# A two-layer decoder trunk: state-space output tables computed on VectorE into tiles of their own, table parts three steps apart, and Toeplitz gathers and V loads spread over a feed-forward stage

## The chip, the cores and the metric

One core of one Trainium2 chip runs the whole program. The metric is the device time of one execution in microseconds (us). Lower is better.

## The reference

Two layers act on x (256 rows of 1024 numbers, fp32). Each layer is a half-step SwiGLU feed-forward (ffn), a token mixer, a second ffn, and a gated embedding (ple). Layer 0 mixes with differential attention, layer 1 with a diagonal state-space model (ssm) and a gated linear unit (glu). Every sub-layer norms its input and its output.

```python
for i in range(2):
    x = x + 0.5 * rmsnorm(swiglu(rmsnorm(x, g[0]), ffn_w_in[i, 0], ffn_w_out[i, 0]), g[1])
    h = rmsnorm(x, g[2])
    m = diff_attention(h, ...) if i == 0 else s5_glu(h, ...)
    x = x + rmsnorm(m, g[3])
    x = x + 0.5 * rmsnorm(swiglu(rmsnorm(x, g[4]), ffn_w_in[i, 1], ffn_w_out[i, 1]), g[5])
    gate = sigmoid(rmsnorm(x, g[6]) @ ple_w_gate[i])
    x = x + rmsnorm(gate * (p[i] @ ple_w_proj[i]), g[7])
# in s5_glu, per group of 16 channels, with 64 complex states a = exp(lam * dt):
#   state = a * state + b_bar @ u ;  y = Re(c @ state) + d * u
```

## The kernel before, in words

**Stages and threads.** The eight stages are ffn(0,0), attention, ffn(0,1), ple(0), ffn(1,0), ssm with glu, ffn(1,1), ple(1). The 256 rows of x are two halves of 128, each worked on by a Python generator, thread 0 and thread 1 (`b` = 0 and 1). A step of a thread uses one weight tile. Thread 0 runs 4 to 7 steps ahead (`lags`), so that both use a tile while it is in SBUF. A scheduler orders the instructions on each engine once, when the program is built; on the chip each engine keeps that order. A block under `high_priority(offset=-800)` is placed with low priority, where an engine seems free.

**Weights.** A weight tile of 128x1024 fp32 is loaded by SP into one of three `raw` buffers. ScalarE rounds it to `hi` (L136), VectorE makes `lo = raw - hi` (L138). There are nine pairs of `hi` and `lo` (NB). A product takes three TensorE matmuls: hi·hi, lo·hi, hi·lo (L312 to L314). Each thread does two such triples of 128x512 with a tile, so a tile is 12 matmuls.

**Around a norm.** `post_norm` takes squares on ScalarE, a reciprocal root on GpSimd (`v_pn`, then `r_pn`, L323 and L327), and then adds to x on VectorE (L387). `pre_norm` transposes x on TensorE (`xT_ps`, L349) and evacuates with ScalarE (`xThi`) and VectorE (`xTlo`, L332). In ple, `mple` is gate times projection and `ygpnple` that times the gain, both on VectorE.

**Tables of the ssm.** While thread 1 runs through ffn(0,1), ple(0) and ffn(1,0), the main loop calls the generator `ssm_tables` at every second step. First come small tables on VectorE: powers of `a` (`ar`, `ai`), `er`, `ei`, then `br`, `bi`. Then, for each of eight group pairs `gp`:
- the v part: six products of 128x512 on GpSimd give `vr`, `vi`; four small GpSimd operations fill `cp`; TensorE transposes `vr`, `vi` (`v_ps`) in two sets of four and multiplies them with `cp` (`m_ps`); the results go to `v_d` in DRAM and to `msb`.
- the o part: six more GpSimd products give `or`, `oi`, in the same two SBUF buffers (tags `vr` and `vi`), stored to `o_d`.

After that `msb` gets a diagonal added (`db`, `dg`), is written to `m_d`, and eight DMAs from the GpSimd queue gather the Toeplitz table: `t_d <- m_d`, 512 KB each, in pieces of 512 bytes. When the generator ends, `load_v` loads four V tiles from `v_d`, 512 KB each, in one go. The ssm stage reads V, `t_d` and `o_d`.

Of the kernel before, what the change touches and what calls it, by code (L numbers as in the profile page):

```python
# [9 lines left out]
F32 = mybir.dt.float32  # L10
# [6 lines left out]
P = 128  # L17
# [49 lines left out]
STAGES = [("ffn", 0, 0), ("attn",), ("ffn", 0, 1), ("ple", 0),  # L67
          ("ffn", 1, 0), ("ssm",), ("ffn", 1, 1), ("ple", 1)]
TABLE_EVERY = OPT.get("every", 3)
PREPARE_AT = 36  # L70
EARLY = 24
LAMBDA_INIT = 0.8 - 0.6 * math.exp(0.0)
# [75 lines left out]
def trunk(ctx, tc, x, p, norm_g, ffn_w_in, ffn_w_out, attn_w_qkv, attn_w_o, attn_lam, attn_subln_g,  # L148
          rel_bias, ssm_lam_re, ssm_lam_im, ssm_log_dt, ssm_b_re, ssm_b_im, ssm_c_re, ssm_c_im, ssm_d, ssm_w_glu,
          ssm_b_glu, ple_w_proj, ple_w_gate, out):  # L150
    nc = tc.nc
# [21 lines left out]
    def bank(tag, name):  # L173
        return ps_extra["pool"].tile([P, 512], F32, tag=tag, name=name)
# [75 lines left out]
    if any(st[0] == "ssm" for st in stages):  # L250
        v_d = dram.tile([8, P, 1024], F32, name="v_d")
# [3 lines left out]
        t_d = dram.tile([P, 8, 1024], F32, name="t_d")  # L255
# [13 lines left out]
    plan = {}  # L269
# [9 lines left out]
    W = Weights(nc, raw_pool, split_pool, specs)  # L279
# [5 lines left out]
    def flat(u):  # L285
        return [u] if isinstance(u, int) else [a for e in u for a in flat(e)]
# [419 lines left out]
    ssm = {}  # L706
# [59 lines left out]
    def ssm_tables(pool, keep):  # L766
        lam, rho = ssm["lam"], ssm["rho"]
        v = nc.vector
        cnt = [0]

        def tmp(nm):
            return pool.tile([P, 32], F32, tag=f"s_{nm}", name=f"st_{nm}", bufs=1)
# [3 lines left out]
        n, y, z2, ps, pc = tmp("n"), tmp("y"), tmp("z2"), tmp("ps"), tmp("pc")  # L776
# [81 lines left out]
        for nm, src in (("re", ssm_b_re), ("im", ssm_b_im)):  # L858
            t = pool.tile([P, 32, 16], F32, tag="v" + nm[0], name=f"braw{nm}", bufs=1)
# [18 lines left out]
        for nm, src in (("re", ssm_c_re), ("im", ssm_c_im)):  # L878
            ct = pool.tile([P, 4, 8, 16], F32, tag=f"c{nm}", name=f"c{nm}", bufs=1)
            csrc = src[0].rearrange("(a g) h p -> (g h) a p", g=8)  # L880
            for hf in range(2):
# [3 lines left out]
                pt = bank("a1", f"c_ps{nm}{hf}")  # L885
# [15 lines left out]
        a4 = [t.rearrange("p k (q g) -> p q g k", q=4) for t in (ar, ai)]  # L901
        shp = [P, 4, 8, 16]

        def products(out_r, out_i, ar_, ai_, br_, bi_, nm):
            g = nc.gpsimd
            t = pool.tile([P, 512], F32, tag="pt", name=f"pt{nm}", bufs=1).rearrange("p (q k h) -> p q k h", q=4, k=8)
            g.tensor_tensor(out_r, ar_, br_, ALU.mult)
            g.tensor_tensor(t, ai_, bi_, ALU.mult)
            g.tensor_tensor(out_r, out_r, t, ALU.subtract)
            g.tensor_tensor(out_i, ai_, br_, ALU.mult)  # L910
            g.tensor_tensor(t, ar_, bi_, ALU.mult)
            g.tensor_tensor(out_i, out_i, t, ALU.add)

        zt = pool.tile([16, 112], F32, tag="vr", name="zt", bufs=1)
# [3 lines left out]
        for gp in range(8):  # L918
            vr = pool.tile(shp, F32, tag="vr", name=f"vr{gp}", bufs=1)
            vi = pool.tile(shp, F32, tag="vi", name=f"vi{gp}", bufs=1)  # L920
            A = [t[:, :, gp, 0:8].broadcast_to(shp) for t in a4]
            B = [t[:, :, gp:gp + 1, :].broadcast_to(shp) for t in b4]
            products(vr, vi, *A, *B, f"v{gp}")
            for e in range(2):
                sl = slice(64 * e, 64 * e + 64)
                nc.gpsimd.tensor_copy(cps[0][sl, :, e, :], c_re[sl, :, gp, :])
                nc.gpsimd.tensor_scalar(cps[1][sl, :, e, :], c_im[sl, :, gp, :], -1.0, None, ALU.mult)
            for i in range(2):
                vt = pool.tile([P, 2, 4, 64], F32, tag="cn", name=f"vt{gp}{i}", bufs=1)
                pt = bank("a0", f"v_ps{gp}{i}")  # L930
                for j in range(4):
                    q, ri = 2 * i + j // 2, j % 2
                    nc.tensor.transpose(pt[:, j * P:(j + 1) * P],
                                        (vr, vi)[ri][:, q].rearrange("p k h -> p (k h)"), ident)
                nc.scalar.copy(vt.rearrange("p e a n -> p a e n"), pt.rearrange("p (a e n) -> p a e n", a=4, e=2))
                nc.sync.dma_start(v_d[gp].rearrange("p (e a n) -> p e a n", e=2, n=64)[:, :, 4 * i:4 * i + 4, :], vt)
            mp = bank("a1", f"m_ps{gp}")
            for ri in range(2):
                for q in range(4):
                    nc.tensor.matmul(mp[32 * q:32 * q + 32, 0:P], cps[ri][:, q].rearrange("p e h -> p (e h)"),  # L940
                                     (vr, vi)[ri][:, q].rearrange("p k h -> p (k h)"), start=ri == 0, stop=ri == 1,
                                     skip_group_check=True)
            mt = work.tile([P, P], F32, tag="gnat", name=f"mt{gp}", bufs=1)
            nc.scalar.copy(mt, mp[:, 0:P])
            mp2 = bank("a0", f"m2_ps{gp}")
            nc.tensor.transpose(mp2[:, :P], mt, ident)
            nc.scalar.copy(msb[:, gp].rearrange("p e q h -> p q e h"), mp2[:, :P].rearrange("p (q e h) -> p q e h", q=4, e=2))
            yield
            o_r = pool.tile(shp, F32, tag="vr", name=f"or{gp}", bufs=1)
            o_i = pool.tile(shp, F32, tag="vi", name=f"oi{gp}", bufs=1)  # L950
            A = [t[:, :, gp, 1:9].broadcast_to(shp) for t in a4]
            C = [t[:, :, gp:gp + 1, :].broadcast_to(shp) for t in cs]
            products(o_r, o_i, *A, *C, f"o{gp}")
            for e in range(2):
                for ri, t in enumerate((o_r, o_i)):
                    nc.sync.dma_start(o_d[gp, ri * 64:ri * 64 + 64, e, :],
                                        t[64 * e:64 * e + 64].rearrange("p q t h -> p (q t h)"))
            yield

        m16 = msb.rearrange("p g e q h -> p (g e q) h")  # L960
        for q in range(4):
# [5 lines left out]
            v.tensor_tensor(db, db, ident[0:16, 0:16].rearrange("p (o h) -> p o h", o=1).broadcast_to([16, 16, 16]), ALU.mult)  # L967
            mq = msb.rearrange("p g e q h -> p (g e) q h")[0:16, :, q, :]
            v.tensor_tensor(mq, mq, db, ALU.add)
        yield 1  # L970
        for k in range(8):
            nc.gpsimd.dma_start(m_d[:, :, 7 + k, :], m16[16 * k:16 * k + 16])
        yield 2
        for s_ in range(8):
            nc.gpsimd.dma_start(t_d[16 * s_:16 * s_ + 16].rearrange("i g (c x) -> i (g c) x", x=P),
                              m_d.rearrange("i g k o -> i g (k o)")[:, :, 16 * s_:16 * s_ + P])
            yield 2


    def ssm_u(b):  # L980
# [238 lines left out]
    has_ssm = any(st[0] == "ssm" for st in stages)  # L1219
    pre = {"gen": None, "n": 0, "every": TABLE_EVERY}  # L1220

# [12 lines left out]
    def tables_step():  # L1234
        if pre["gen"] is not None:
            try:
                with tc.high_priority(offset=-PRE_OFFSET[min(pre["n"], len(PRE_OFFSET) - 1)]):
                    pre["every"] = next(pre["gen"]) or TABLE_EVERY
                pre["n"] += 1
# [5 lines left out]
    def load_v():  # L1245
        for pr in range(2):
            ssm["V", pr] = [ssm["pool"].tile([P, 1024], F32, tag=("bglu", "vx")[pr], name=f"V{pr}{j}", bufs=2)
                            for j in range(2)]
            for j in range(2):
                nc.sync.dma_start(ssm["V", pr][j], v_d[2 * pr + j])  # L1250

    def end_tables():
        while pre["gen"] is not None:
# [34 lines left out]
    while any(s_ == "run" for s_ in state):  # L1288
        b = 0 if state[0] == "run" and (steps[0] - steps[1] < lag[0] or state[1] != "run") else 1
        if state[b] != "run":  # L1290
            b = 1 - b
        try:
            if next(th[b]) == "ssm":
                state[b] = "join"
            steps[b] += 1
        except StopIteration:
            state[b] = "done"
        if b == 0 and steps[0] == PREPARE_AT:
            attn_prepare()
            if has_ssm:  # L1300
                ssm_exp()
        if not started and steps[1] >= attn_steps and (state[1] != "run" or steps[1] > attn_steps):
            started = True
            start_tables()
        if started and b == 1 and steps[1] % pre["every"] == 0:
            tables_step()
        if has_ssm and "pool" in ssm and ("V", 0) not in ssm and W.next >= plan[("ssm",)][0][0] - OPT["vl"]:
            load_v()
        if state == ["join", "join"]:
            end_tables()  # L1310
            if ("V", 0) not in ssm:
                load_v()
            pool = ssm["pool"]
            both = [proj(b, 1, plan[("ssm",)][0]) for b in range(2)]
            for b in (0, 1, 0, 1, 0, 1):
                next(both[b], None)
            ssm_core(pool, *plan[("ssm",)][1:3])
            W.order = lambda: tc.issue_after(W.last.ins)
            state = ["run", "run"]
# [24 lines left out]
```

## Time and profile before

| what | value |
|---|---|
| median of 3 runs | 1120.79 us (1118.37 to 1122.93) |
| the profiled execution: its time | 1120.96 us |
| its span, first to last instruction | 1119.2 us |
| TensorE (PE) busy | 1043.0 us (93%) |
| VectorE (DVE) busy | 696.5 us (62%) |
| ScalarE (ACT) busy | 553.8 us (49%) |
| GpSimd (POOL) busy | 255.4 us (23%) |

PE is the engine that the program fills; the time it sits idle, or runs at less than its granted full clock, is what can be won. Shares are means over the span, and stages differ much: POOL is nearly idle in most of the span and busy from 420 to 640 us. ffn(0,1) runs from about 350 to 535 us, ple(0) to about 600 us, ffn(1,0) to about 795 us, the core of the ssm to about 850 us.

### The profile page before, as it was taken

The numbers are of one execution on the slowest core, as the hardware profiler recorded it, in microseconds if no ns is written. First come the engines' busy times: TensorE is split into PE (matmuls) and PEld (weight loads), VectorE is DVE, ScalarE is ACT, GpSimd is POOL, SyncE is SP. The second block draws the span as 40 slices with busy tenths as digits, with TensorE's granted clock in tenths as the row PEclk, the third lists the DMA queues.
The fourth block names the chain that finished last, engine by engine and source line by source line (L and its number), as shares of the span: only waits on it lengthen the run. The fifth ranks groups of instructions, "written<-read, shape, count | busy, mean of one in ns | idle before, by whom it ended". The sixth has DMA issues, their size and how long they took to land. (4 is left out here: it accounts for less than half of the span.)

```text
span 1119.2 us, 14344 instructions
## 1 busy us (share of the span) xinstructions
PE 1043.0 (93%) x5123; PEld 835.7 (75%) x5123; DVE 696.5 (62%) x1011; ACT 553.8 (49%) x875; POOL 255.4 (23%) x315
## 2 busy tenths in 40 slices
PE   7999999999989999999778998999768899999996
PEld 5888888787766887777556886888546778888885
DVE  6656645688568986554686663654377676555464
ACT  6545444566655544443464543543335465444454
POOL 1002100100011018887788530000131010000001
PEclk9999999999999999999898999999989999999999
DMA  9656656476366777666564778766874647665651
GB/s 328 197 149 189 210 189 201 144 235 201 106 144 185 207 179 233 208 194 216 157 181 118 211 236 307 247 198 206 225 308 166 204 148 215 188 186 180 198 168 57
DMA packets 119816, 218.62 MB, mean 195 GB/s; under 512 B 25025, under 2 KB 43489, under 8 KB 119745
## 3 DMA queue, kind: packets, MB, share of 16 engines
q1 hardware_dynamic: 116864, 211.71, 60.9%
q0 software_dynamic: 1824, 5.33, 1.7%
q8 instruction: 40, 0.66, 0.2%
q10 hardware_dynamic: 1056, 0.66, 0.2%
q14 instruction: 32, 0.25, 0.1%
HBM read 205.13 MB, written 16.74 MB: 198 GB/s over the span
## 5 line engine op out<-in xcount | busy, mean ns | idle before, releaser
L138 DVE TENSOR_TENSOR lo<-raw,hi 128x1024 fp32r<-128x1024 f32 x332 | 429.6, 1301 | 266.3 <-ACT hi L136 264.7
L136 ACT CAST hi<-raw 128x1024 fp32r<-128x1024 f32 x332 | 347.3, 1052 | 327.1 <-PE up L314 106.5
L312 PE MATMUL up<-hi,xThi 128*128 128x512 f32 x704 | 279.3, 400 | 5.2 <-ACT hi L136 2.9
L313 PE MATMUL up<-lo,xThi 128*128 128x512 f32 x704 | 278.8, 397 | 1.5 <-DVE lo L138 1.4
L314 PE MATMUL up<-hi,xTlo 128*128 128x512 f32 x704 | 279.0, 400 | 0.0
L312 PEld LDWEIGHTS up<-hi,xThi 128*128 128x128 f32 x704 | 133.9, 190 | 34.8 <-ACT xThi L331 4.3
L313 PEld LDWEIGHTS up<-lo,xThi 128*128 128x128 f32 x704 | 134.1, 190 | 31.1 <-DVE lo L138 3.6
L314 PEld LDWEIGHTS up<-hi,xTlo 128*128 128x128 f32 x704 | 133.5, 191 | 28.1 <-issue 0.4
L312 PE MATMUL dn<-hi,hThi 128*128 128x512 f32 x352 | 139.2, 396 | 0.0
L313 PE MATMUL dn<-lo,hThi 128*128 128x512 f32 x352 | 138.5, 393 | 0.0
L314 PE MATMUL dn<-hi,hTlo 128*128 128x512 f32 x352 | 138.4, 394 | 0.0
L312 PEld LDWEIGHTS dn<-hi,hThi 128*128 128x128 f32 x352 | 66.8, 190 | 14.2 <-issue 0.6
L314 PEld LDWEIGHTS dn<-hi,hTlo 128*128 128x128 f32 x352 | 66.7, 190 | 14.3 <-issue 0.2
L313 PEld LDWEIGHTS dn<-lo,hThi 128*128 128x128 f32 x352 | 66.8, 190 | 13.6
L331 ACT ACTIVATE xThi<-xT_ps,gT 128x128 fp32r<-128x128 f32 x112 | 38.2, 368 | 59.2 <-PE xT_ps L349 58.3
L323 POOL TENSOR_SCALAR v_pn<-sspn,sspn 128x1 f32<-128x1 f32 x8 | 3.4, 422 | 246.8 <-ACT junkpn L380 244.7
L335 ACT CAST hThi<-hT_ps 128x512 fp32r<-128x512 f32 (+1 forms) x48 | 26.4, 550 | 56.2 <-PE hT_ps L459 56.0
L336 DVE TENSOR_TENSOR hTlo<-hT_ps,hThi 128x512 fp32r<-128x512 f32 (+1 forms) x48 | 30.8, 643 | 36.8 <-ACT hThi L335 36.7
L332 DVE SCALAR_TENSOR_TENSOR xTlo<-xT_ps,gT,xThi 128x128 fp32r<-128x128 f32 x112 | 36.1, 344 | 26.0 <-ACT xThi L331 25.5
L349 PE MATMUL xT_ps<-ident,x 128*128 128x128 f32 x112 | 30.3, 305 | 22.4 <-DVE xTlo L332 9.9
L349 PEld LDWEIGHTS xT_ps<-ident,x 128*128 128x128 f32 x112 | 16.2, 150 | 32.6 <-DVE xTlo L332 13.4
L456 DVE SCALAR_TENSOR_TENSOR h<-up,r_pre,sg 128x512 f32<-128x512 f32 (+1 forms) x48 | 33.6, 702 | 10.7 <-ACT sg L454 7.3
(360 smaller groups left out, 1319.5 us busy)
## 6 DMA issues: line engine op xcount, KB each, us to landing
raw<-in_ffn_w_in_dram SPq DMA_DIRECT2D x160, 512.0 KB, 4.4
raw<-in_ffn_w_out_dram SPq DMA_DIRECT2D x88, 512.0 KB, 3.9
raw<-in_attn_w_qkv_dram SPq DMA_DIRECT2D x24, 512.0 KB, 4.4
raw<-in_ffn_w_in_dram SPq DMA_DIRECT2D x32, 256.0 KB, 3.7
raw<-in_ple_w_gate_dram SPq DMA_DIRECT2D x16, 512.0 KB, 3.5
raw<-in_ssm_w_glu_dram SPq DMA_DIRECT2D x16, 512.0 KB, 4.1
gain<-in_norm_g_dram SPq DMA_DIRECT2D x8, 512.0 KB, 4.8
raw<-in_attn_w_o_dram SPq DMA_DIRECT2D x8, 512.0 KB, 4.2
```

Source lines behind the costliest of these rows:

```text
L136: nc.scalar.copy(hi, raw)
L138: (nc.gpsimd if n in self.on_pool else nc.vector).tensor_tensor(lo, raw, hi.bitcast(F32), ALU.subtract)
L312: nc.tensor.matmul(out_ap, st_hi, w_hi, start=start, stop=False)
L313: nc.tensor.matmul(out_ap, st_hi, w_lo, start=False, stop=False)
L314: nc.tensor.matmul(out_ap, st_lo, w_hi, start=False, stop=stop)
L323: nc.gpsimd.tensor_scalar(v, parts[0], parts[1], eps, ALU.add, ALU.add)
L331: return (nc.scalar.activation(hi, psum, AF.Copy, scale=scale).ins, nc.vector.scalar_tensor_tensor(lo, psum, scale, hi.bitcast(F32), ALU.m ...
L332: nc.vector.scalar_tensor_tensor(lo, psum, scale, hi.bitcast(F32), ALU.mult, ALU.subtract).ins)
L335: nc.scalar.copy(hi, psum)
L336: nc.vector.tensor_tensor(lo, psum, hi.bitcast(F32), ALU.subtract)
L349: marks[b].append(nc.tensor.transpose(pt, xb[:, k * P:(k + 1) * P], ident).ins)
L456: nc.vector.scalar_tensor_tensor(h[:, :w], up_, r, sg[:, :w], ALU.mult, ALU.mult)
```

## The change

The o products go to VectorE, into tiles `or`, `oi`, `po` of their own. Table parts are three thread steps apart instead of two. The writes of `m_d` wait in the program until 24 weight tiles of ffn(1,0) are asked for, the eight gathers stand four steps apart, and each has a one-element GpSimd copy ahead of it that reads the newest weight tile (the tile from which it takes its pace). The V loads come one per step, once the next weight tile is within 16 of the end of ffn(1,0). The ring that GpSimd's DMAs use is set to 8192 bytes.

```diff
+V_AHEAD = 16
+TD_FROM = 24
...
-        def products(out_r, out_i, ar_, ai_, br_, bi_, nm):
-            g = nc.gpsimd
-            t = pool.tile([P, 512], F32, tag="pt", name=f"pt{nm}", bufs=1).rearrange("p (q k h) -> p q k h", q=4, k=8)
+        def products(g, tag, out_r, out_i, ar_, ai_, br_, bi_, nm):
+            t = pool.tile([P, 512], F32, tag=tag, name=f"pt{nm}", bufs=1).rearrange("p (q k h) -> p q k h", q=4, k=8)
...
-            products(vr, vi, *A, *B, f"v{gp}")
+            products(nc.gpsimd, "pt", vr, vi, *A, *B, f"v{gp}")
...
-            yield
-            o_r = pool.tile(shp, F32, tag="vr", name=f"or{gp}", bufs=1)
-            o_i = pool.tile(shp, F32, tag="vi", name=f"oi{gp}", bufs=1)
+            yield 3
+            o_r = pool.tile(shp, F32, tag="or", name=f"or{gp}", bufs=1)
+            o_i = pool.tile(shp, F32, tag="oi", name=f"oi{gp}", bufs=1)
-            products(o_r, o_i, *A, *C, f"o{gp}")
+            products(v, "po", o_r, o_i, *A, *C, f"o{gp}")
...
-            yield
+            yield 3
...
-        yield 1
+        while W.next < flat(plan[("ffn", 1, 0)])[0] + TD_FROM:
+            yield 1
         for k in range(8):
             nc.gpsimd.dma_start(m_d[:, :, 7 + k, :], m16[16 * k:16 * k + 16])
         yield 2
+        pace = pool.tile([1, 8], F32, tag="zt", name="pace", bufs=1)
         for s_ in range(8):
-            nc.gpsimd.dma_start(t_d[16 * s_:16 * s_ + 16].rearrange("i g (c x) -> i (g c) x", x=P),
-            yield 2
+            n = max(W.tiles)
+            gate = nc.gpsimd.tensor_copy(pace[:, s_:s_ + 1], W.tiles[n][0].bitcast(F32)[0:1, 0:1])
+            with tc.issue_after(gate.ins):
+              nc.gpsimd.dma_start(t_d[16 * s_:16 * s_ + 16].rearrange("i g (c x) -> i (g c) x", x=P),
                               m_d.rearrange("i g k o -> i g (k o)")[:, :, 16 * s_:16 * s_ + P])
+            yield 4
...
-                nc.sync.dma_start(ssm["V", pr][j], v_d[2 * pr + j])
+                with tc.issue_after(W.last_raw.ins):
+                    nc.sync.dma_start(ssm["V", pr][j], v_d[2 * pr + j])
+                yield
...
-        if has_ssm and "pool" in ssm and ("V", 0) not in ssm and W.next >= plan[("ssm",)][0][0] - OPT["vl"]:
-            load_v()
+        if has_ssm and "pool" in ssm and b == 1 and W.next >= plan[("ssm",)][0][0] - V_AHEAD:
+            ssm.setdefault("loads", load_v())
+            next(ssm["loads"], None)
...
+    nc = _bacc.Bacc("TRN2", target_bir_lowering=False, num_devices=1, dynamic_dma_scratch_size=8192)
```

The order of instructions moves in three places that matter. The first is VectorE early in ffn(0,1), where `lo` rows are weight tiles and the `cm` and `st` rows belong to the small tables. Before:

```order
L138 TENSOR_TENSOR lo_3425<-raw_3422,hi_3424 128x1024
L726 TENSOR_TENSOR ai<-cmu_3260 128x128
L138 TENSOR_TENSOR lo_3459<-raw_3456,hi_3458 128x1024
L717 TENSOR_TENSOR cmsq_3270<-st_ur 128x32
L718 TENSOR_TENSOR cmsq_3270<-st_ui 128x32
L336 TENSOR_TENSOR hTlo_3020<-hT_ps_3329,hThi_3019 128x512
L719 TENSOR_TENSOR st_ur_3268<-cmsq_3270 128x32
L138 TENSOR_TENSOR lo_3478<-raw_3475,hi_3477 128x1024
```

And now (`or`, `oi`, `pto` are the o products):

```order
L140 TENSOR_TENSOR lo_3425<-raw_3422,hi_3424 128x1024
L728 TENSOR_TENSOR ai<-cmu_3260 128x128
L140 TENSOR_TENSOR lo_3459<-raw_3456,hi_3458 128x1024
L909 TENSOR_TENSOR pto_3916<-ai,cim 128x512
L911 TENSOR_TENSOR oi_3915<-ai,cre 128x512
L719 TENSOR_TENSOR cmsq_3270<-st_ur 128x32
L720 TENSOR_TENSOR cmsq_3270<-st_ui 128x32
L338 TENSOR_TENSOR hTlo_3020<-hT_ps_3329,hThi_3019 128x512
L140 TENSOR_TENSOR lo_3478<-raw_3475,hi_3477 128x1024
L910 TENSOR_TENSOR or_3914<-or_3914,pto_3916 128x512
```

All 48 o products stand between the 111th and the 141st `lo` row of the program, ahead of most of the small tables. The last of those (`bi`) stood behind the 132nd `lo` row and now stands behind the 152nd, and the v parts, which read it, start there.

The second place is GpSimd, from the end of a v part on to the next v part; before it is the one ahead of the first `post_norm` of ple(0):

```order
L912 TENSOR_TENSOR vi_4389<-vi_4389,ptv_4390 128x512
L908 TENSOR_TENSOR pto_4483<-ai,cim 128x512
L926 COPY cp_3816<-cre 64x4x16 x2
L927 TENSOR_SCALAR cp_3818<-cim 64x4x16 x2
L907 TENSOR_TENSOR or_4481<-ar,cre 128x512
L910 TENSOR_TENSOR oi_4482<-ai,cre 128x512
L909 TENSOR_TENSOR or_4481<-or_4481,pto_4483 128x512
L911 TENSOR_TENSOR pto_4483<-ar,cim 128x512
L323 TENSOR_SCALAR v_pn_5199<-sspn_5193,sspn_5196 128x1
L912 TENSOR_TENSOR oi_4482<-oi_4482,pto_4483 128x512
L327 TENSOR_TENSOR r_pn_5201<-v_pn_5199,neg_half 128x1
L907 TENSOR_TENSOR vr_4532<-ar,br 128x512
```

Now:

```order
L913 TENSOR_TENSOR vi_4173<-vi_4173,ptv_4174 128x512
L909 TENSOR_TENSOR ptv_4353<-ai,bi 128x512
L927 COPY cp_3816<-cre 64x4x16 x2
L928 TENSOR_SCALAR cp_3818<-cim 64x4x16 x2
L325 TENSOR_SCALAR v_pn_5145<-sspn_5139,sspn_5142 128x1
L329 TENSOR_TENSOR r_pn_5147<-v_pn_5145,neg_half 128x1
L908 TENSOR_TENSOR vr_4351<-ar,br 128x512
L911 TENSOR_TENSOR vi_4352<-ai,br 128x512
L910 TENSOR_TENSOR vr_4351<-vr_4351,ptv_4353 128x512
L912 TENSOR_TENSOR ptv_4353<-ar,bi 128x512
L327 TENSOR_SCALAR v_pre_5184<-ss_5182 128x1
L913 TENSOR_TENSOR vi_4352<-vi_4352,ptv_4353 128x512
```

The o products between two v parts are gone, and `v_pn` and `r_pn` follow each other with no product between.

The third place is VectorE at the end of ple(0), where thread 1 leaves ple and thread 0 is in the transposes of ffn(1,0). Before:

```order
L520 TENSOR_TENSOR mple_5612<-mple_5612,sigple_5610 128x512
L383 TENSOR_TENSOR ygpnple_5616<-mple_5607,gain_5205 128x512
L383 TENSOR_TENSOR ygpnple_5616<-mple_5612,gain_5205 128x512
L138 TENSOR_TENSOR lo_5676<-raw_5673,hi_5675 128x1024
L332 SCALAR_TENSOR_TENSOR xTlo_5483<-xT_ps_5484,gT,xThi_5482 128x128
L332 SCALAR_TENSOR_TENSOR xTlo_5483<-xT_ps_5485,gT,xThi_5482 128x128
L332 SCALAR_TENSOR_TENSOR xTlo_5483<-xT_ps_5484,gT,xThi_5482 128x128
L387 SCALAR_TENSOR_TENSOR x_101<-ygpnple_5616,r_pnple_5625,x_101 128x512
```

Now:

```order
L522 TENSOR_TENSOR mple_5592<-mple_5592,sigple_5590 128x512
L385 TENSOR_TENSOR ygpnple_5596<-mple_5587,gain_5151 128x512
L385 TENSOR_TENSOR ygpnple_5596<-mple_5592,gain_5151 128x512
L140 TENSOR_TENSOR lo_5656<-raw_5653,hi_5655 128x1024
L389 SCALAR_TENSOR_TENSOR x_101<-ygpnple_5596,r_pnple_5605,x_101 128x512 x2
L334 SCALAR_TENSOR_TENSOR xTlo_5463<-xT_ps_5464,gT,xThi_5462 128x128
L334 SCALAR_TENSOR_TENSOR xTlo_5463<-xT_ps_5465,gT,xThi_5462 128x128
```

The two updates of x moved ahead of the `xTlo` rows that thread 0's next transposes need.

## Rows read from the trace of the kernel before

**Rows 1.** The page: its span, and its first part.

```profile
span 1119.2 us, 14344 instructions
PE 1043.0 (93%) x5123; PEld 835.7 (75%) x5123; DVE 696.5 (62%) x1011; ACT 553.8 (49%) x875; POOL 255.4 (23%) x315
```

**Rows 2.** Stretches: busy us (instructions) by engine, granted clock, DMA share, GB/s.

```profile
340.00:480.00 140.00, 134.41 (x661) 106.95 (x660) 106.63 (x225) 67.03 (x88) 59.58 (x53) 1.00 0.68 198
440.00:530.00 90.00, 83.57 (x424) 64.83 (x423) 49.47 (x36) 36.32 (x48) 76.29 (x60) 0.98 0.66 211
530.00:620.00 90.00, 73.91 (x343) 54.72 (x342) 61.76 (x68) 47.63 (x91) 71.40 (x62) 0.89 0.51 148
660.00:700.00 40.00, 36.35 (x155) 28.89 (x154) 17.08 (x19) 13.71 (x16) 7.28 (x10) 0.96 0.84 291
700.00:780.00 80.00, 80.00 (x364) 66.21 (x363) 44.17 (x43) 37.09 (x41) 0.00 (x0) 1.00 0.68 216
```

**Rows 3.** PE's waits: us in total, times, longest us.

```profile
PE xT_ps L349 <- DVE xTlo L332: 9.9, 6, 3.7
PE v_ps L933 <- POOL vi L912: 9.7, 5, 3.5
```

**Rows 4.** PE's timeline: start, us, then in brackets idle before it.

```profile
525.42 0.33 PE L933 MATMUL v_ps<-ident,vi 128*128 128x128 f32 x1 [2.08 <-POOL vi L912]
...
538.78 0.39 PE L312 MATMUL dn<-hi,hThi 128*128 128x512 f32 x1
...
539.92 0.39 PE L314 MATMUL dn<-hi,hTlo 128*128 128x512 f32 x1
544.12 0.69 PE L349 MATMUL xT_ps<-ident,x 128*128 128x128 f32 x2 [3.81 <-DVE x L387]
...
586.40 0.33 PE L933 MATMUL v_ps<-ident,vi 128*128 128x128 f32 x1 [3.47 <-POOL vi L912]
...
603.17 0.47 PE L349 MATMUL xT_ps<-ident,x 128*128 128x128 f32 x1 [3.69 <-DVE xTlo L332]
...
681.87 0.50 PE L312 MATMUL up<-hi,xThi 128*128 128x512 f32 x1 [2.46 <-ACT hi L136]
```

**Rows 5.** POOL's groups, 400 to 700 us: costliest and cheapest product, one `cp`.

```profile
L908 POOL TENSOR_TENSOR ptv<-ai,bi 128x512 f32<-128x512 f32 x8 | 14.5, 1815 | 0.1
...
L910 POOL TENSOR_TENSOR vi<-ai,br 128x512 f32<-128x512 f32 x8 | 11.3, 1407 | 0.3 <-DMA o_d<-oi 0.2
L926 POOL COPY cp<-cre 64x64 f32<-64x64 f32 x14 | 6.6, 472 | 0.3
```

**Rows 6.** DVE: `lo` in two windows (ns min/median/max), and products of 128x512.

```profile
L138 DVE TENSOR_TENSOR lo<-raw,hi x57: 1207/1642/2353, 422.4 to 635.7; 128x1024 fp32r<-128x1024 f32 x57
L138 DVE TENSOR_TENSOR lo<-raw,hi x60: 1216/1225/1228, 918.9 to 1078.5; 128x1024 fp32r<-128x1024 f32 x60
L870 DVE TENSOR_TENSOR brawim<-brawim,gb 128x512 f32<-128x512 f32 x1 | 0.7, 682 | 0.0
L383 DVE TENSOR_TENSOR ygpnple<-mple,gain 128x512 f32<-128x512 f32 x8 | 9.0, 1151 | 0.0
```

**Rows 7.** DMA, 664 to 693 us, then 700 to 780 us, then SP's timeline.

```profile
q0 software_dynamic: 1169, 4.22, 38.2%
t_d<-m_d POOLq DMA_DIRECT2D x8, 512.0 KB, 13.7
raw<-in_ffn_w_in_dram SPq DMA_DIRECT2D x6, 512.0 KB, 10.9
...
raw<-in_ffn_w_out_dram SPq DMA_DIRECT2D x22, 512.0 KB, 4.2
...
804.37 0.33 SPq L115 DMA_DIRECT2D hi<-t_d  x1
```

**Rows 8.** Stores of the o part: issues with us to landing, and SP's timeline.

```profile
o_d<-oi SPq DMA_DIRECT2D x16, 128.0 KB, 2.5
514.48 1.09 SPq L956 DMA_DIRECT2D o_d<-oi  x2
```

More of the change, by code (lines that the diff above doesn't have):

```diff
@@ L1306, in trunk @@
             tables_step()
-        if has_ssm and "pool" in ssm and ("V", 0) not in ssm and W.next >= plan[("ssm",)][0][0] - OPT["vl"]:
-            load_v()
+        if has_ssm and "pool" in ssm and b == 1 and W.next >= plan[("ssm",)][0][0] - V_AHEAD:
+            ssm.setdefault("loads", load_v())
+            next(ssm["loads"], None)
         if state == ["join", "join"]:
             end_tables()
-            if ("V", 0) not in ssm:
-                load_v()
+            for _ in ssm.setdefault("loads", load_v()):
+                pass
             pool = ssm["pool"]
@@ L1331 @@
     from concourse.bass_utils import run_bass_kernel_spmd as _run
-    nc = _bacc.Bacc("TRN2", target_bir_lowering=False, num_devices=1)
+    nc = _bacc.Bacc("TRN2", target_bir_lowering=False, num_devices=1, dynamic_dma_scratch_size=8192)
     arrays, args = {}, []
```

## The prediction

> **What bounds the kernel now.** The first view is the page: PE is busy 93% of the span, the next engine 62% [rows 1]. PE's work does not change here, so a gain can only come from time in which PE idles or runs below its full clock. The second view, the stretches, says where that is in the part that the change touches [rows 2]. From 700 to 780 us PE has no idle time. From 440 to 530 us it idles 6.4 us of 90; from 530 to 620 us 16.1 us, and there the granted clock is 0.89; from 660 to 700 us 3.65 us. PE has two clock levels, 1.2 and 2.4 GHz, so a mean of 0.89 over 90 us is work lost worth 9.9 us, 0.98 over 90 us is 1.8 us, and 0.96 over 40 us is 1.6 us. The sums of idle and lost clock are 8.2, 26.0 and 5.3 us.
>
> The third view, PE's waits and its timeline, says why [rows 3, 4]. From 440 to 530 us PE waits for GpSimd to end `vi`: the waits for `vi` are 9.7 us in all, of which 3.47 us lie at 586 us, so 6.2 us lie here. From 530 to 620 us, ple(0), the waits are for x (3.81 us at 544) and for `xTlo` (3.69 us at 603), and once more for `vi`. At 682 us PE waits for a rounded weight tile, which waits for its load.
>
> **A check of what GpSimd needs.** There are twelve groups of eight products, of 1.41 to 1.82 us, mean 1.57 us [rows 5]. PE's matmuls follow each other at (539.92 - 538.78) / 5 = 0.228 us [rows 4], so a weight tile of twelve is 2.7 us. `vr` and `vi` are single buffers: a new v part starts when the second `v_ps` set has read the old one. In the old order 11 products and four `cp` stand between that and the next `vi`: 11 x 1.57 + 4 x 0.47 = 19.1 us. PE's matmuls in its order between the same two points come to 16 to 17 us at that pace. The lack, 2 to 3 us a round, is of the size of the waits found, the longest 2.08 us. So GpSimd sets the pace there.
>
> **The change, part by part.**
>
> *GpSimd loses 48 products.* Between the second `v_ps` set and the next `vi` there are now 5 products, 7.9 us. I count PE's matmuls in the new order for the seven rounds: 9.4, 9.4, 6.0, 8.7, 7.3, 7.8 and 8.6 us. The first two, which lie in ffn(0,1), have room. So the 6.2 us before ple(0) go, and with them the lost clock of that stretch: -8.0 us. It could be nothing if GpSimd were late again (price 0 to -8); I take -8, since room of 1.5 us a round replaces a lack of 2.
>
> *ple(0) keeps most of its waits.* The later start of the tables puts five v rounds into ple(0), so GpSimd is as full there as before and VectorE as slow (a `lo` beside it 1.64 us, alone 1.225 us [rows 6]). The wait for x at 544 us should go: `v_pn` and `r_pn` are now neighbours, which takes out a product and shortens the chain by over 2 us, and PE's matmuls ahead of that transpose become 4.8 us where they were 4.2. But the third v round lacks 1.9 us by the count above and has `r_pn` and `v_pre` in its queue, together 1.5 us: 3.4 us of wait take its place. In the middle of ple(0) thread 1's first `xTlo` now stands behind two `mple` and one `ygpnple`; by slow rows of about 1.5 us this is some 4.4 us (two waits). One v round more: 1.0 us. At the end, two updates of x stand ahead of the `xTlo` that PE needs at what was 603 us: 3.69 + 2 x 1.6 (an update beside GpSimd, twice 1.15 to 1.6) less 0.9 us of more matmuls ahead = 6.0 us. The sum is 14.8 us where there were 16.1, and one wait fewer to lower the clock, 8.7 us where there were 9.9: -2.5 us. Bounds: all waits halve, -12; or each 1 us longer, +4. I stay near zero since the rows show the same contention.
>
> *VectorE gains 48 products.* A product of 128x512 from SBUF took 0.68 us with GpSimd idle, 1.15 us in the slow rows [rows 6]. GpSimd has no products at that place any more, so 0.68: 48 x 0.68 = 32.6 us. VectorE is free for 33.4 us from 340 to 480 us [rows 2], and gets back some 22 x 0.42 = 9 us as 22 `lo` no longer run beside GpSimd. So it fits, with nothing to spare. In the new order the 20 more `lo` rows ahead of the last small table are 20 x 2.7 = 55 us of room. What hides it is the lead of the weights: nine pairs less a lag of six leaves three tiles, 8.2 us, less 2.3 us for rounding and `lo`, 5.9 us. If the cover were gone each us more would be a us of PE. New waits: `or` and `oi` have one buffer, so VectorE waits for the stores. Two issues of 1.09 us together and 2.5 us to land [rows 8] are 3.6 us; the order leaves 3.3 to 5.2 us of VectorE work between. Behind such a wait stand `lo` and `h`, so PE. Price 0 to +8; I take +1.5.
>
> *Gathers.* Eight gathers and four V loads met the weights at 665 to 692 us: six weight loads took 10.9 us to land where 4.2 us is usual, and the gathers alone held 38% of 29 us of all DMA engines, 1.4 us each [rows 7]. Paced four steps apart, that is 1.4 us in 10.9; the DMA share of that stage goes from 0.68 [rows 2] to 0.81. The wait at 682 us and its clock go: -4.9 of 5.3 us. The gate is a one-element copy on GpSimd, which has nothing else to do then. The 24th tile is asked for at about 655 us; the last gather stands 34 steps later, about 750 us, and `t_d` is first read at 804 us [rows 7], so lateness is covered by 50 us. Bounds -5.3 and 0.
>
> *V loads.* Four loads of 512 KB, one beside each of four weight loads late in ffn(1,0). For 11 us the DMA moves twice 512 KB per 2.7 us, 384 GB/s, near what the gathers drew. A weight can land some 2 us late, and the lead covers that. 0 to +4; I take +0.5. The steps three apart only move when parts stand, which the counts hold already. A smaller ring could make a GpSimd DMA wait; none is hurried any more, so 0. If its cover went, the `m_d` writes would delay the gathers, which have their 50 us.
>
> Sum: -8.0 - 2.5 + 1.5 - 4.9 + 0.5 = -13.4 us from the profiled execution's 1120.96 us (0.17 us over the median), **1107.5 us**. Half a per cent, 5.6 us, is about what a measurement of this kernel tells from no change.
>
> **Rivals.**
>
> *A, the forecast:* waits for `vi` ahead of ple(0) and the wait at 682 us gone, ple(0) nearly as it was. 1103 to 1112 us. Chance 0.42.
>
> *B, ple(0) heals too:* with half its products GpSimd may be done sooner, and VectorE's slow rows there with it. Half of 14.8 + 8.7 us more goes: 1107.5 - 11.7 = 1096 us. For it: every wait there follows a slow row. Against it: the order keeps five v rounds there. 0.18.
>
> *C, pacing spreads the wait:* a paced gather still shares the engines with a weight load. If that load takes twice 4.2 us, it is followed by 2.3 us of rounding and `lo`, 10.7 us against three `raw` buffers or 8.2 us. Eight times 2.5 us, less the lead of 5.9 us once, is 14 us: 1121.5 us, no change. Against it: 1.4 us of engine time per gather, not 4.2. The Trainium skill, "DMA: Bandwidth & Descriptors", section on queues, rings and completion order, speaks for it: each DMA engine takes turns between queues a packet at a time, so a gather on GpSimd's queue and a weight on SP's would get equal turns. The trace agrees in kind: 38.2% went to GpSimd's queue while both were full. By that rule alone this rival's 1121.5 us would be the sum. 0.13.
>
> *D, VectorE waits for its stores:* 16 waits of 0.7 us are 11 us, less 5.9 us of lead, and the clock after them: 1113 to 1117 us. 0.14.
>
> *E, slower, VectorE becomes the bound:* if operands that repeat along the row make a product cost 1.55 us, like the slow rows, 48 x 0.87 = 42 us are added where nothing is to spare. Less the 5.9 us of lead and the 9 us that the lighter `lo` give back, PE loses 27 us: 1135 us. The gain is gone at (13.4 + 14.9) / 48 = 0.59 us more, 1.27 us a product, and it is slower by 5.6 us at 1.39 us. Against it: the slow rows all lie beside GpSimd's products. 0.06.
>
> *F, the gathers were not the cause:* the wait at 682 us stays, the rest as forecast: 1112.5 us. Against it: weight loads that take 10.9 us. 0.07.
>
> **How the numbers follow.** The likeliest is A, 1107.5 us. From 1095 to 1119 us holds A, B, D and F and leaves out C and E, 0.19. Faster by over 0.5%, under 1115.2 us: A, B, F and half of D, 0.74. Within: C and the other half, 0.20. Slower: E, 0.06.
>
> **What would show it.** In the new profile: no wait of PE for `vi` ahead of the first `post_norm` of ple(0); VectorE over 0.9 busy for some 110 us from 350 us on, its products near 0.68 us, hardly a wait for `o_d`; waits for `xTlo` and `vi` in ple(0) of 12 to 17 us; gathers some 11 us apart with weight loads landing under 6 us; full clock at 680 us. The prediction is wrong if PE waits for `lo` in ffn(0,1), or if the waits of ple(0) change by more than 5 us.

## The result and the profile after

The median fell from 1119.58 us (4 runs) to **1104.51 us** (4 runs, 1103.48 to 1107.96): a ratio of 0.9864, 95% interval 0.9844 to 0.9884. The profiled execution fell from 1120.96 to 1104.74 us, so by 16.2 us where the sum of terms said 13.4. Later, on another chip, the same kernel stood at 1101.86 us beside 1119.27 us for the kernel before, 0.9848 (0.9825 to 0.9871). Each ratio below is to the kernel before, run beside it on the same chip.

The page's head after [rows 1]:

```profile
span 1102.9 us, 14355 instructions
PE 1038.8 (94%) x5123; PEld 835.2 (76%) x5123; DVE 705.6 (64%) x1059; ACT 554.9 (50%) x875; POOL 189.2 (17%) x275
```

To see where the 16 us lie, the start of the same matmul of the same weight tile is looked up in both timelines. It is some 10.6 us earlier at the end of ffn(0,1) and at the end of ple(0), 16 to 16.7 behind the gathers, 16.3 at the end. So the stretches are cut at the same work. Before, in the columns of [rows 2]:

```profile
340.00:530.00 190.00, 181.59 (x892) 143.85 (x891) 133.66 (x242) 86.44 (x113) 101.41 (x85) 0.99 0.68 202
530.00:617.00 87.00, 70.91 (x328) 52.25 (x327) 58.91 (x66) 45.78 (x88) 68.85 (x60) 0.88 0.52 151
617.00:692.00 75.00, 71.30 (x320) 57.42 (x319) 41.24 (x49) 31.87 (x41) 24.99 (x30) 0.98 0.81 258
```

After:

```profile
340.00:519.40 179.40, 174.33 (x832) 140.23 (x831) 148.14 (x290) 82.54 (x103) 37.17 (x37) 1.00 0.73 217
519.40:606.40 87.00, 72.61 (x384) 52.54 (x385) 55.13 (x66) 49.66 (x98) 63.89 (x66) 0.90 0.48 148
606.40:676.00 69.60, 69.60 (x324) 57.36 (x323) 43.79 (x54) 35.95 (x45) 16.45 (x22) 1.00 0.78 227
350.00:460.00 110.00, 109.94 (x508) 90.33 (x507) 101.45 (x205) 53.11 (x63) 1.80 (x2) 1.00 0.76 227
```

The first stretch is 10.6 us shorter, ple(0) as long as before, the stretch of the gathers 5.4 us shorter with no idle time and full clock. In the last row VectorE is 0.92 busy while PE lacks nothing: the o products are hidden. In ple(0) PE idles less, 14.4 us where it was 16.1, yet its length is the same: it now holds 44 of the v rounds' transposes (`v_ps`) where 26 stood, the work of two rounds more.

PE's timeline after, the longest waits ahead of and in ple(0) [rows 4]:

```profile
485.45 0.33 PE L934 MATMUL v_ps<-ident,vr 128*128 128x128 f32 x1 [1.71 <-POOL vr L910]
488.86 0.33 PE L934 MATMUL v_ps<-ident,vi 128*128 128x128 f32 x1 [1.37 <-POOL vi L913]
537.34 0.47 PE L934 MATMUL v_ps<-ident,vi 128*128 128x128 f32 x1 [2.79 <-POOL vi L913]
559.17 0.50 PE L314 MATMUL gtple<-hi,xThi 128*128 128x512 f32 x1 [2.06 <-ACT xThi L333]
563.43 0.48 PE L351 MATMUL xT_ps<-ident,x 128*128 128x128 f32 x1 [2.68 <-DVE xTlo L334]
594.06 0.47 PE L351 MATMUL xT_ps<-ident,x 128*128 128x128 f32 x1 [4.71 <-DVE xTlo L334]
```

VectorE's o products, the slowest group and a plain one [rows 6], then a paced gather on POOL:

```profile
L908 DVE TENSOR_TENSOR or<-ar,cre 128x512 f32<-128x512 f32 x8 | 5.6, 696 | 5.8 <-DMA o_d<-or 5.8
L909 DVE TENSOR_TENSOR pto<-ai,cim 128x512 f32<-128x512 f32 x8 | 5.5, 684 | 0.0
```

```profile
667.31 1.23 POOL L979 COPY pace<-hi 1x1 f32<-1x1 f32 x1 [9.10 <-ACT hi L138]
668.49 0.76 POOL L981 DMA_DIRECT2D t_d<-m_d  x1
```

### The profile page after: what moved, and what is told of

Same layout as the page of the kernel before. It is cut to its first block, busy times and chain, and to the rows that moved or that the text cites. A ratio compares the mean times of both kernels' runs of the same rounds, so it can differ in the third digit from the quotient of the medians.

```text
span 1102.9 us, 14355 instructions
## 1 busy us (share of the span) xinstructions
PE 1038.8 (94%) x5123; PEld 835.2 (76%) x5123; DVE 705.6 (64%) x1059; ACT 554.9 (50%) x875; POOL 189.2 (17%) x275
## 4 chain that ended last, share of the span: by engine, by line
PE 55%; issue 20%; DVE 10%; DMA 7%; POOL 4%; ACT 3%; SPq 1%; DVEq 0%; POOLq 0%; ACTq 0%
PE up L315 8%; PE up L314 8%; PE up L316 8%; PE dn L316 5%; PE dn L314 5%; PE dn L315 5%; DVE lo L140 3%; DMA o_d<-or 2%; PE qkvat L314 2%; PE qkvat L315 2%; PE qkvat L316 2%; DMA raw<-in_ffn_w_in_dram 2%; ACT hi L138 1%; PE xT_ps L351 1%; PE hT_ps L461 1%
## 5 line engine op out<-in xcount | busy, mean ns | idle before, releaser
L140 DVE TENSOR_TENSOR lo<-raw,hi 128x1024 fp32r<-128x1024 f32 x332 | 413.0, 1251 | 229.5 <-ACT hi L138 227.7
L351 PE MATMUL xT_ps<-ident,x 128*128 128x128 f32 x112 | 30.1, 300 | 16.7 <-DVE xTlo L334 9.3
L314 PE MATMUL qkvat<-hi,xThi 128*128 128x512 f32 x96 | 38.1, 397 | 0.3 <-ACT xThi L333 0.3
```

Of the source, the lines that this page charges most:

```text
L140: (nc.gpsimd if n in self.on_pool else nc.vector).tensor_tensor(lo, raw, hi.bitcast(F32), ALU.subtract)
L314: nc.tensor.matmul(out_ap, st_hi, w_hi, start=start, stop=False)
L351: marks[b].append(nc.tensor.transpose(pt, xb[:, k * P:(k + 1) * P], ident).ins)
```

## The experiments

| kernel | median us | before, same chip | ratio to before (95%) |
|---|---|---|---|
| paced gathers and V loads alone | 1116.21 | 1120.71 | 0.9954 (0.9937 to 0.9970) |
| o on VectorE alone | 1109.16 | 1120.71 | 0.9901 (0.9871 to 0.9931) |
| changed, gathers in a burst | 1104.93 | 1120.71 | 0.9853 (0.9825 to 0.9881) |
| changed, o on GpSimd in own tiles | 1130.44 | 1120.71 | 1.0076 (1.0050 to 1.0102) |
| changed, again | 1101.86 | 1119.27 | 0.9848 (0.9825 to 0.9871) |
| changed, gathers in a burst, again | 1101.07 | 1119.27 | 0.9839 (0.9815 to 0.9863) |
| changed, V loads in a burst | 1101.20 | 1119.27 | 0.9840 (0.9815 to 0.9864) |
| changed, temporaries exchanged | 1115.20 | 1119.27 | 0.9963 (0.9947 to 0.9980) |
| changed, o products twice | 1101.01 | 1120.58 | 0.9833 (0.9810 to 0.9857) |
| changed, v products cut | 1084.39 | 1120.58 | 0.9678 (0.9664 to 0.9692) |
| changed, `er`, `ei` late | 1099.35 | 1120.58 | 0.9812 (0.9797 to 0.9826) |
| changed, five v rounds held | 1096.70 | 1120.79 | 0.9777 (0.9751 to 0.9802) |

### The two halves apart

The kernel before with the edits of the gathers and V loads alone (the hunks on `V_AHEAD`, `TD_FROM`, `pace`, `yield 4`, `load_v` and the ring), and the kernel before with the o products on VectorE alone (with the smaller ring too, so the ring is in both halves and no run tells what it does by itself):

```diff
-            products(o_r, o_i, *A, *C, f"o{gp}")
+            products(v, "po", o_r, o_i, *A, *C, f"o{gp}")   # tags or, oi; parts two steps apart
```

> The kernel before, with the paced gathers and V loads alone; the o products stay on GpSimd. Theory, that the gathers' burst cost what the trace of before shows at 664 to 693 us (3.65 us idle, 1.6 us of clock, and by the drift of the two traces some 6 us): 5 to 6.5 us less than before, no idle time of PE at the gathers, ple(0) as before. Rival C, that pacing only spreads the wait: 0, with many small waits for hi from 660 to 740 us. Rival, that the stage of the gathers was freed by the lighter GpSimd ahead of it: 0 to 2 us less, and the wait for hi stays.

> The kernel before with the o products on VectorE in their own tiles and nothing else: parts two steps apart, gathers and V loads as before. Theory: 9 to 10.5 us less than before, since the spacing of parts matters little once GpSimd has half the work. Rival, that the spacing of three steps is half of it: 3 to 6 us less than before, with waits for vi in ffn(0,1).

By the ratios they gave 0.46% and 0.99%, 5.2 and 11.1 us: together the change's whole gain. The first is what its theory said, the second half a microsecond above the 9 to 10.5 of its own. Rival C falls: the paced gathers leave PE one wait of 0.46 us between 620 and 780 us. The second kernel keeps its wait at the gathers. That the spacing of three steps moves nothing ahead of the V loads is seen in the traces: the second kernel (two steps) and the changed kernel with the gathers in a burst (three) have the same rows in the same order on GpSimd all through, and on PE, VectorE and ScalarE up to the V loads. Behind these the two cannot be told apart by the steps, since the V loads differ too.

### Which burst hurts

The changed kernel with the eight gathers issued together, or with the four V loads together (`load_v` as in the kernel before). The diff is that of the gathers:

```diff
-        while W.next < flat(plan[("ffn", 1, 0)])[0] + TD_FROM:
             yield 1
...
-            gate = nc.gpsimd.tensor_copy(pace[:, s_:s_ + 1], W.tiles[n][0].bitcast(F32)[0:1, 0:1])
-            with tc.issue_after(gate.ins):
...
-            yield 4
+            yield 2
```

> The changed kernel with the eight gathers in one burst as before (V loads still one by one). Theory, that the two parts are independent: 5 to 6.5 us more than the changed kernel, 9 to 10 less than before, and PE waits for hi during the burst. Rival F, that the gathers were not the cause: the time of the changed kernel, within 1 us.

> The changed kernel with the gathers in one burst, once more, beside the changed kernel itself. The first time its trace lost 4.6 us at the burst and its total stood within 2 us of the changed kernel. Theory, that the pacing is worth its 4 us and the stages behind it are even: 3 to 5 us more than the changed kernel. Rival, that most of it is given back between 780 and 890 us, where PE waits for the ssm chain and the clock follows the waits: within 2 us.

> The changed kernel with the four V loads in one go as before, gathers paced. Theory, that without the gathers beside them the four loads are covered by the lead of the weights: within 1.5 us of the changed kernel. Rival, that the V loads were the harmful half of the burst: 3 to 5 us more, PE waits for hi behind them.

> The changed kernel once more, to stand beside the next three on one chip: 0.986 of the kernel before, 15 to 16 us less.

Neither burst costs anything that the total shows: 0.9853 and 0.9839 for the gathers, 0.9840 for the V loads, beside 0.9848. For the gathers the rivals held both times, for the V loads the theory; these now come at 725 us, beside the last of the gathers. So the step on the gathers was wrong in one point. The source of the kernel with o on VectorE alone differs from the one with the gathers in a burst only in how the V loads are issued (and in the steps), and it is 0.48% slower, 5.4 us (4.2 by the medians). Its SP and its ScalarE, first the issue of the V loads beside the gathers, which start at 655.16 us, then the waits of 640 to 700 us, then PE's wait:

```profile
655.05 2.16 SPq L1251 DMA_DIRECT2D V<-v_d  x4
```

```profile
ACT hi L138 <- DMA raw<-in_ffn_w_in_dram: 28.2, 14, 11.5
```

```profile
671.14 0.50 PE L314 MATMUL up<-hi,xThi 128*128 128x512 f32 x1 [2.02 <-ACT hi L138]
```

The second run of the gathers in a burst, whose V loads come at 710 us, one by one:

```profile
709.66 0.33 SPq L1252 DMA_DIRECT2D V<-v_d  x1
```

```profile
ACT hi L138 <- DMA raw<-in_ffn_w_in_dram: 25.9, 14, 5.0
```

```profile
682.49 0.66 PE L461 MATMUL hT_ps<-ident,h 128*128 128x128 f32 x4 [1.72 <-DVE h L458]
```

The sum of the waits of `hi` is nearly the same; the longest is 11.5 us in one and 5.0 in the other. The lead that the prediction worked out is 5.9 us. It covers 5.0 and not 11.5. By these rows the cover was longer than 5.9, since PE waits only 2.0 us behind the 11.5, and 2.46 us behind a wait of 9.6 us in the kernel before [rows 4].

What the V loads add is clear in the total, less so at the place itself. Followed by the start of the same matmul from 658 to 684 us of the changed kernel, the kernel before loses 6.1 us there, the one with o on VectorE alone 4.8, the two runs of the gathers in a burst 3.6 and 2.0. So the gathers alone still make PE wait: `h` stands on VectorE behind a `lo` whose weight tile landed late. The two runs differ by the granted clock behind that wait, 0.84 and 1.00 from 680 to 690 us. Part of such a loss is gone at the end, but the changed kernel's own two traces also part by 2.7 us behind 850 us, so this is inside their spread. Two more things are not separated. With the V loads the scheduler's order moved too (of PE's matmuls between 676 and 696 us, and of `lo`, `h` and `hi` rows from 655 us on). And the V loads stand in SP's own queue ahead of the weights, so it may be their place as well as their number. That taking the gathers away would do as well is seen only with the V loads at another place; the kernel before with the V loads alone moved was not run.

One row bears on the smaller ring, too. In the kernel before the eight issues of the gathers follow each other; in the three traces with the smaller ring and the gathers in a burst, the eighth stands 1.65 to 2.65 us behind the seventh and waits for nothing that the profile shows.

### Engine or buffers

```diff
-            products(v, "po", o_r, o_i, *A, *C, f"o{gp}")
+            products(nc.gpsimd, "po", o_r, o_i, *A, *C, f"o{gp}")
```

> The changed kernel with the o products back on GpSimd, but in their own tiles and three steps apart. Theory, that GpSimd's busy time per round sets the pace: the gain of the earlier stretches goes, 8 to 10 us more than the changed kernel, 5 to 7 less than before; waits for vi over 1.5 us ahead of ple(0). Rival, that the shared buffers and the two steps were the limit, not the engine: within 3 us of the changed kernel.

Both sides missed: it is slower than the kernel before. With buffers of their own the o products run ahead of all v parts, where VectorE is at its fullest. Two stretches, then PE's waits of the whole trace, nearly all of which lie in the first:

```profile
340.00:460.00 120.00, 97.80 (x402) 75.54 (x400) 113.19 (x199) 40.94 (x55) 76.54 (x61) 0.91 0.60 162
460.00:575.00 115.00, 110.67 (x598) 85.08 (x598) 61.26 (x50) 55.24 (x80) 86.47 (x76) 0.99 0.68 215
```

```profile
PE hT_ps L461 <- DVE h L458: 10.7, 5, 3.5
...
PE up L315 <- DVE lo L140: 8.8, 7, 2.4
```

From 340 to 460 us PE idles 22 us, 19 of them because VectorE is late beside GpSimd (a `lo` up to 2.34 us where it takes 1.22, and most small-table rows slower too). Behind it, where GpSimd has only v rounds to do, they run 13 to 16 us apart, 22 to 32 in the kernel before, and PE idles 4.3 us in 115. That fits the first step, by which GpSimd's queue was the limit of the v rounds [rows 3]. What the change of engine buys besides is that no GpSimd product stands beside VectorE's full stretch.

### The v rounds earlier, beside the o products

The temporaries are exchanged, so that the o products share one with the small tables (their last stands at 501 us where it was 444) and the v parts start at 429 us where it was 485:

```diff
-            products(nc.gpsimd, "pt", vr, vi, *A, *B, f"v{gp}")
+            products(nc.gpsimd, "po", vr, vi, *A, *B, f"v{gp}")
-            products(v, "po", o_r, o_i, *A, *C, f"o{gp}")
+            products(v, "pt", o_r, o_i, *A, *C, f"o{gp}")
```

> The changed kernel with the two temporaries exchanged: the o products share theirs with the small tables (so they stand behind these), the v products have one of their own. v parts start some 45 us earlier, most ahead of ple(0), o products later, beside them. Theory, that the waits of ple(0) come from GpSimd's and VectorE's products there: ple(0) loses half of its idle time and of its lost clock, 8 to 12 us, some 4 of it given back as waits for lo; 3 to 8 us less than the changed kernel. Rival, that VectorE beside GpSimd becomes the bound in ffn(0,1), as it was ahead of 460 us with the o products on GpSimd: 0 to 10 us more than the changed kernel, with waits of PE for lo over 1 us each from 430 to 530 us.

The rival holds, and worse than it said, some 13 us over the changed kernel. From 430 to 530 us VectorE's groups are:

```profile
L140 DVE TENSOR_TENSOR lo<-raw,hi 128x1024 fp32r<-128x1024 f32 x26 | 41.2, 1590 | 10.2 <-ACT hi L138 10.2
L910 DVE TENSOR_TENSOR or<-or,pto 128x512 f32<-128x512 f32 x7 | 8.2, 1165 | 0.0
```

The same product that takes 0.684 us in the changed kernel takes 1.165 us in the mean here, beside GpSimd's v products. PE's waits for `lo` are up to 2.0 us, those for `h` up to 5.3. The order that the change happened to get, o products first and v rounds behind, is what keeps them apart.

### VectorE's load doubled

```diff
-            products(v, "po", o_r, o_i, *A, *C, f"o{gp}")
+            for r_ in range(2):
+                products(v, "po", o_r, o_i, *A, *C, f"o{gp}{r_}")
```

> The changed kernel with the 48 o products done twice on VectorE: 32.6 us more work for it, on 30 more weight tiles, and so the v parts start some 40 us later (in the order one round stands in ffn(0,1), two in ple(0), five in ffn(1,0)). Theory, that VectorE has about 1.5 us to spare a tile there and that the waits of ple(0) come from the rounds in it: no waits of PE for lo over 1 us, ple(0) loses a third of its idle time, 0 to 8 us less than the changed kernel. Rival E, that VectorE is at its bound there: PE waits for lo and h from 460 to 540 us, 8 to 20 us more.

PE has no wait for `lo` over 0.5 us from 400 to 700 us, and the total loses nothing. VectorE is over 0.9 busy in two stretches; the third row is ple(0), cut at the same work as above:

```profile
340.00:460.00 120.00, 117.75 (x545) 96.00 (x544) 114.77 (x244) 58.80 (x74) 4.30 (x8) 1.00 0.71 208
460.00:540.00 80.00, 74.62 (x341) 60.25 (x340) 73.16 (x112) 34.44 (x46) 25.05 (x21) 0.96 0.70 216
511.50:597.80 86.30, 72.07 (x371) 52.30 (x370) 58.05 (x75) 46.80 (x94) 72.09 (x71) 0.90 0.53 162
```

The one long wait of PE in the first two is 5.06 us for the first `vr`, at 525 us, which the tables' later start explains. Rival E is out. The theory's second half missed: ple(0) holds five rounds, not two, and idles 14.2 us, as in the changed kernel.

### What ple(0) waits for

GpSimd's v products from the third pair on are cut to an eighth:

```diff
+            if gp < 2:
                 products(nc.gpsimd, "pt", vr, vi, *A, *B, f"v{gp}")
+            else:
...
+                g.memset(vr, 0.5); g.memset(vi, 0.25)
+                g.tensor_tensor(t[s], A[1][s], B[1][s], ALU.mult)      # s: one of eight k
+                g.tensor_tensor(vr[s], vr[s], t[s], ALU.subtract)
+                g.tensor_tensor(vi[s], vi[s], t[s], ALU.add)
```

> The changed kernel with GpSimd's v products from the third group pair on cut to an eighth and filled with constants (part of the table is left out); transposes, matmuls, stores and the o products stay. Theory, that what PE still waits for in ple(0) is GpSimd's products, by vi and by VectorE's slow rows beside them: the idle time of PE in ple(0), 14.4 us, falls to 6 or less and its clock loss of 8 us to 4 or less, 10 to 14 us less than the changed kernel. Rival, that ple(0) waits for its own norms and gates: 1 to 4 us less.

It is 1.7 to 1.9% faster than the changed kernel, about 20 us, more than expected. Its ple(0), then its VectorE from 525 to 605 us, then the same groups of the changed kernel:

```profile
530.00:620.00 90.00, 88.33 (x487) 68.29 (x487) 58.99 (x94) 58.71 (x111) 34.27 (x69) 1.00 0.65 196
```

```profile
L140 DVE TENSOR_TENSOR lo<-raw,hi 128x1024 fp32r<-128x1024 f32 x22 | 26.9, 1231 | 16.6 <-ACT hi L138 16.6
L334 DVE SCALAR_TENSOR_TENSOR xTlo<-xT_ps,gT,xThi 128x128 fp32r<-128x128 f32 x32 | 10.4, 344 | 7.1 <-ACT xThi L333 7.1
...
L522 DVE TENSOR_TENSOR mple<-mple,sigple 128x512 f32<-128x512 f32 x4 | 2.6, 697 | 1.6 <-ACT sigple L518 1.6
```

```profile
L140 DVE TENSOR_TENSOR lo<-raw,hi 128x1024 fp32r<-128x1024 f32 x15 | 22.2, 1488 | 8.5 <-ACT hi L138 8.5
L334 DVE SCALAR_TENSOR_TENSOR xTlo<-xT_ps,gT,xThi 128x128 fp32r<-128x128 f32 x27 | 8.9, 343 | 12.3 <-ACT xThi L333 12.1
L522 DVE TENSOR_TENSOR mple<-mple,sigple 128x512 f32<-128x512 f32 x4 | 5.7, 1468 | 3.3 <-ACT sigple L518 3.3
```

The idle time of ple(0) falls from 14.4 to 1.7 us and the clock is full; 12.7 us of idle time and 8.1 of clock are the whole 20. So nearly all of what is left there comes with GpSimd's products, directly (`vi`) or through VectorE. How much is the products' time and how much the order is not separated: with the shorter products the scheduler also put `xTlo` ahead of the `ygpnple` that it stood behind in the changed kernel. The rows show which instructions suffer: `mple` and `lo`, whose two large operands lie in SBUF, go from 0.70 to 1.47 and from 1.23 to 1.49 us; `xTlo`, which reads PSUM, stays at 0.34. The Trainium skill, "SBUF — State Buffer", section "SBUF: two separate sides", says that a VectorE instruction with two SBUF inputs and a GpSimd instruction that reads SBUF share a port as an exclusive lock; by that rule these can be made to wait and `xTlo` cannot, and the trace agrees.

### Two ways to get the rounds out of ple(0)

First, `er` and `ei`, which only the ssm reads, are made behind the o parts (their block of code is moved). The scheduler then spreads the rounds otherwise: one begins ahead of ple(0), four lie in it and three behind it, where the changed kernel has two, five and one.

> The changed kernel with the small tables er and ei, that only the ssm stage reads, made behind the o parts. br and bi are ready 20 weight tiles sooner, yet the scheduler puts one v round in ffn(0,1), two or three in ple(0) and the rest in ffn(1,0), where PE does not idle. Theory, as in the kernel with the o products twice: fewer rounds in ple(0), a third to a half of its idle time and clock loss goes, 4 to 10 us less than the changed kernel. Rival, that GpSimd and VectorE in ffn(1,0) then make PE wait there or late gathers do: 0 to 8 us more.

Within what was expected, though the intervals touch: 0.9812, four to six us under the changed kernel. Second, the last five rounds are held by data until thread 0 has begun ffn(1,0); the o parts move ahead of them, and the gathers start six tiles later and three steps apart:

```diff
+            while gp == 3 and W.next < flat(plan[("ffn", 1, 0)])[0] + 8:
+                yield 1
...
+            if gp == 3:
+                gate = nc.gpsimd.tensor_copy(hold[:, 0:1], W.tiles[max(W.tiles)][0].bitcast(F32)[0:1, 0:1])
+                with tc.issue_after(gate.ins):
+                    products(nc.gpsimd, "pt", vr, vi, *A, *B, f"v{gp}")
```

The four rounds behind that one follow it.

> The changed kernel with the o parts ahead of all v parts in the program (which alone moves nothing on the engines), the first three v rounds where they were, and the other five held by a one-element GpSimd copy of a weight tile until ffn(1,0) has begun; the gathers start six tiles later and stand three steps apart. Theory, that a v round is dear in ple(0), where PE waits for every step of the norms, and free in ffn(1,0), where it has a lead of weights: ple(0) as with the cut products, no new wait of PE from 600 to 780 us, 12 to 18 us less than the changed kernel. Rival, that what ple(0) sheds comes back in ffn(1,0), as waits for lo beside GpSimd's products or behind the gathers, four of which now stand together: within 5 us of the changed kernel.

0.9777, about 24 us under the kernel before and 8 to 10 under the changed one: the best version. The gain is some half of what theory said. Its ffn(0,1), ple(0) and the first part of ffn(1,0), cut at the same matmuls as the three stretches of the changed kernel (179.4, 87.0 and 69.6 us):

```profile
339.70:522.50 182.80, 177.75 (x832) 142.40 (x831) 147.96 (x290) 82.14 (x103) 37.02 (x37) 0.98 0.71 214
522.50:591.80 69.30, 61.68 (x289) 45.22 (x289) 46.52 (x66) 43.31 (x83) 25.76 (x36) 0.98 0.52 159
591.80:671.20 79.40, 79.40 (x420) 61.64 (x419) 46.48 (x44) 40.87 (x60) 45.98 (x45) 1.00 0.70 200
```

ple(0) is 17.7 us shorter: idle time and lost clock fall from 14.4 + 8.7 to 7.6 + 1.4 us, and PE's rows of v rounds in it from 137 to 41, of 25 a round. ffn(1,0), where PE is full in both, is 9.8 us longer: the work that left ple(0) is done here, and it is not free, since no idle time takes it up. So moving a round took some 4.6 us from ple(0) and gave some 2.6 to ffn(1,0) (estimates, by 96 rows or 3.8 rounds). ffn(0,1) is 3.4 us longer, with a clock of 0.98; no run says why. The other 3.3 us of this pair of traces lie behind the gathers, about as much as two traces of the changed kernel differ there.

## Why the prediction held, point by point

- **GpSimd loses 48 products, -8.0 us.** The place and the cause were right: that stretch is 10.6 us shorter. But the step as put, that all 6.2 us of `vi` waits ahead of ple(0) go, was not: a wait for `vr` of 1.71 and one for `vi` of 1.37 us stay. Idle time and clock there give 5.2 us (8.4 + 1.9 where now 5.1 + 0). The other 5.4 us are PE work of v rounds that the later start carried out of ffn(0,1), so they are moved and not won.
- **ple(0), -2.5 us.** Its length did not change, 87 us; its idle time is 14.4 us where 14.8 were forecast, its clock loss 8.7 us as forecast. The 3.4 us that this saves (16.1 + 10.4 before) are eaten by the rounds moved in, which the prediction put at 1.0 us. Of the single waits, the one for x went as said. The third round costs 2.79 + 0.70 (3.4 said), thread 1's first transposes 2.06 + 2.68 (4.4 said), the end 4.71 (6.0 said).
- **VectorE gains 48 products, +1.5 us.** Mis-sized: 0. Products took 0.684 us (0.68 said). The stores took 3.5 and 4.1 us to land (2.5 said); VectorE waited 6.6 us for them in all, and no PE wait came of it. Doubling the products cost nothing either, so "nothing to spare" was too dark: the scheduler stretches them over more tiles. Rivals D and E did not occur.
- **Gathers, -4.9 us.** Measured -5.4 us in the stretch, and -5.2 alone. The size was right and the owner only in part: it is the meeting of gathers and V loads that costs what the total shows; the gathers alone, all at once, cost 2.0 and 3.6 us at their place and nothing that the total shows. The weights near the paced gathers landed in up to 7.5 us (under 6 said), and none kept PE waiting. Rival C falls. Of rival F, the wait at 682 us is gone, but its doubt that the gathers by themselves were the cause fits the totals.
- **V loads, +0.5 us.** 0.
- **The steps three apart.** The prediction said that they "only move when parts stand"; up to the V loads they move nothing.
- **The rest**, from 676 us on, is 0.3 us.

So -10.6 - 0.0 - 5.4 - 0.3 = -16.3 us of span stand against the -13.4 of the sum; 2 us of the difference are the two costs that did not come. That the sum lies so near is partly luck: the first term came out 2.6 us better and ple(0) 2.5 us worse, and the same moved rounds stand behind both. Neither of the prediction's signs of being wrong came: PE has no wait for `lo` over 0.5 us, and the idle time of ple(0) changed by 1.7 us. Rival B did not occur in this change, but its mechanism is real: with the rounds out of the way, ple(0) does heal.

## What to carry to other kernels

A helper engine's work is priced by what stands beside it: the same v rounds took 17.7 us of a stage where every norm and gate is waited for, and 9.8 us of a stage where PE is full. Work that moves is not work that is saved: cut both traces at the same work before a stretch is called shorter. Look for transfers that meet, not for the largest one: with two groups at once the longest wait for a load was 11.5 us, with one of them 5.0, and the total could not tell that one from none. Before a gain is put down to a spacing or a step count, compare the order of instructions with and without it.

## What was not expected of the hardware

The same 48 products, ahead of the v rounds both times, made the kernel 0.8% slower than before on GpSimd and 1.5% faster on VectorE, though VectorE is by far the fuller of the two: what they do to the neighbour costs more than their own time. And the granted clock went down with waits of at most 4.71 us each: ple(0) with PE idle 14.4 us of 90 was granted 0.91 of full clock (two levels, 1.2 and 2.4 GHz), with 1.7 us idle 1.00, so each us of wait there went with some 0.6 us more (8.1 / 14.4).
